# Summing the modulation over 128 rows on VectorE, by 32x32 block transposes and adds, in place of TensorE transposes

## The chip, the cores and the metric

The kernel runs on one core of a Trainium2 chip. The metric is the device time of one execution in microseconds (us), taken as the median over several runs. A profile and a trace of one further execution are at hand.

## The reference

Two transformer blocks run one after the other, each of depth 2, on 256 tokens of width 1024 in float32. The second block is conditioned: in each of its two layers a vector `c` (for the latent stream x) and a vector `c_ctx` (for the context stream h) are turned into nine modulation vectors of 1024 numbers, three for each sublayer (shift, scale and gate):

```
sc = jax.nn.silu(c)
scc = jax.nn.silu(c_ctx)
...
mod_x = (sc @ w_mod[l] + b_mod[l]).reshape(b_, N_MOD, 1, D_MODEL)
mod_h = (scc @ w_mod[l] + b_mod[l]).reshape(N_MOD, 1, D_MODEL)
...
y = adaln_in(s, g_pre, mod[..., 3 * j, :, :], mod[..., 3 * j + 1, :, :])   # rmsnorm(s) * (1 + scale) + shift
return adaln_out(s, swiglu(y, wg, wu, wd), g_post, mod[..., 3 * j + 2, :, :], FFN_RES)
```

`w_mod[l]` is 1024 x 9216. The product of a single row with it is what the change touches. Everything else (projections, attention of several kinds, SwiGLU layers) stays as it is.

## The kernel before

**The large products.** Weights come from HBM as granules of 512 KB by `nc.sync.dma_start` (tile `raw`, 4 buffers). ScalarE copies each half to a rounded float32r tile and VectorE subtracts to get the remainder (tile `hl`, 5 buffers, function `split`). TensorE multiplies in three passes (`mm3`). In the FFN of block 1 one column step is 48 matmuls of 256 columns (`mm_c`); in the FFN of block 2 the columns of both streams are mostly made together (`both`, 24 matmuls of 512 columns for gate and 24 for up). The row products are groups of `mm_f` or `mm_r`.

**The modulation.** `mod_units` makes the modulation vectors of layer `l` from column block `lo` to `hi`. For each block `i` of 1024 columns, eight tiles of `w_mod` (128 x 1024, tile `modraw`, loaded by POOL's queue into four buffers) are multiplied by a per-partition scalar and accumulated on VectorE, once for x and once for h (`part`, tile `modacc`, 128 x 1024 each, two sets). This leaves for each column 128 partial sums, one in each partition. `total` then sums over the partitions: for each half of 512 columns, four TensorE transposes into a PSUM bank (tile `mm_t`), a VectorE reduction of 128x4 from 128x512, and a VectorE add of the bias. The result lies in `modt` with the column on the partition. There are 18 blocks (4 and 5 in each layer), two streams and two halves: 72 calls of `total` and 288 transposes.

The four calls of `mod_units` are spread over the FFNs: blocks 0 and 1 of layer 0 in the FFN of block 1's first layer, blocks 2 and 3 in that of its second layer, blocks 4 to 8 in the first FFN of block 2, blocks 0 to 3 of layer 1 in its second FFN, and blocks 4 to 8 of layer 1 in its third. `fin` and `put` follow each third block. The heads of the sublayers (`pre_units`) and the rewriting of the rows' buffers wait for them.

**The order.** All work is written as units in five streams (`sx`, `sat`, `sh`, `smod`, `stot`). The function `run` plans with modelled durations (`PE_NS`, `Engine.ns`) and emits every engine's instructions in the planned order, which is then fixed. A unit with an entry in `PE_NS` takes TensorE and a PSUM bank; one without is VectorE or ScalarE work. Steps of one engine compete by class (`CLASS`): 1 if nothing else is said, 2 for the weight split, which becomes 0 when less than `SLACK` = 2500 ns of TensorE work is prepared, and 3 for `part`. In the planner's model a VectorE instruction of n elements costs 68 + n/0.96 ns. `t2k` is a ring of four buffers of 128x512 float32, used by the FFNs for the activated gate (`sg`, `gu`) and by others.

Of the kernel before, what the change touches and what calls it, by code (L numbers as in the profile page):

```python
# [11 lines left out]
F32 = mybir.dt.float32  # L12
# [3 lines left out]
ALU = mybir.AluOpType  # L16
AX = mybir.AxisListType
PSUM = bass.MemoryType.PSUM

P = 128  # L20
# [34 lines left out]
MOD_LAT = 1000.0  # L55
# [69 lines left out]
class Gran:  # L125


    def __init__(self, ap, kind):
# [7 lines left out]


PE_NS = {"col": 5760, "proj": 5760, "rope1": 5760, "half1": 2880, "half2": 2880, "wide1": 5450, "wide2": 5450, "joint": 5450, "row": 1365, "row_add": 1365, "row_last": 1365,
         "tr": 450, "total": 440, "put": 110, "rbc": 430, "start1": 30, "start2": 300, "r1": 650, "r2": 650, "r3": 430,
         "hstat": 1650, "happly": 3400, "s1": 650, "s2": 870, "s3": 650, "rope2": 860, "kcvc2": 650, "wst": 430,  # L140
         "sc2": 1730, "sc1": 870, "trp": 430, "trp2": 870, "avf": 1300, "avc": 860, "bst": 320, "gm": 1040, "bapply": 1740}
BANKS = {"row": 0, "wide1": 2, "wide2": 0, "row_add": 1, "row_last": 0, "half2": 0, "happly": 2, "sc2": 2, "bapply": 2, "trp2": 2}
# [67 lines left out]
class Chained:  # L210

    name, chained, bonus = "v", True, BONUS
# [247 lines left out]
def tile_two_blocks(ctx: ExitStack, tc, io, out):  # L460
    nc = tc.nc
    meter = Meter()
    V, A = Engine(nc.vector, "v", meter), Engine(nc.scalar, "a", meter)
    PE, G = Engine(nc.tensor, "pe", meter), nc.gpsimd
# [6 lines left out]
    sm = ctx.enter_context(tc.tile_pool(name="sm", bufs=4))  # L471
# [4 lines left out]
    ident = cst[:, C_ID:C_ID + 128]  # L476
# [5 lines left out]
    vecs = cpool.tile([P, 306], F32, name="vecs")  # L482
    V_N1, V_N2, V_RET, V_SB, V_SUB = 0, 16, 32, 40, 48
    V_C, V_PRE, V_POST, V_BM = 50, 66, 114, 162
    sc = cpool.tile([P, 2, KT], F32, name="sc")
    modt = [cpool.tile([P, 2, 72], F32, name=f"modt{l}") for l in range(DEPTH)]
# [16 lines left out]
    def t2k(shape, name):  # L503

        return wk.tile(shape, F32, tag="t2k", name=name, bufs=4)

    def t1k(shape, name):
        return wk.tile(shape, F32, tag="t1k", name=name, bufs=3)
# [4 lines left out]
    def mm_ps(shape, name):  # L513
        return ps_mm.tile(shape, F32, tag="mm", name=name)

    def st_ps(name):
        return ps_mm.tile([P, 512], F32, tag="mm", name=name)
# [440 lines left out]
    stot = Stream("tot", -2)  # L958
# [77 lines left out]
    u = sx.add("none", start0)  # L1036
# [9 lines left out]
    def mod_units(l, lo, hi, pace, after, buffers):  # L1046


        wm = io["w_mod_2"][l]
        M = {}  # L1050
        g0, g1 = 8 * lo, 8 * hi

        def load(g):
            if g < g1:
                i, k = divmod(g, 8)
                G.dma_start(M["raw"][g % len(M["raw"])], wm[k * P:(k + 1) * P, i * D:(i + 1) * D])  # L1056

        def part(g, c):
            i, k = divmod(g, 8)

            def fn():
                if g == g0 and c == 0:
                    M["raw"], M["acc"] = buffers()
                    for n in range(len(M["raw"])):
                        load(g + n)
                r = M["raw"][g % len(M["raw"])]
                if k == 0:
                    V.tensor_scalar_mul(M["acc"][i % 2][c], r, sc[:, c, k:k + 1])
                else:
                    V.scalar_tensor_tensor(M["acc"][i % 2][c], r, sc[:, c, k:k + 1], M["acc"][i % 2][c],  # L1070
                                           op0=ALU.mult, op1=ALU.add)
                if c == 1:
                    load(g + len(M["raw"]))
            return fn

        def total(i, c, e):
            def fn():
                ps = mm_ps([P, 4, P], "mm_t")
                m = modt[l][:, c, 8 * i + 4 * e:8 * i + 4 * e + 4]
                for j in range(4):  # L1080
                    PE.transpose(ps[:, j, :], M["acc"][i % 2][c][:, (4 * e + j) * P:(4 * e + j + 1) * P], ident)

                def tail():
                    yield V
                    V.tensor_reduce(m, ps, axis=AX.X, op=ALU.add)
                    at = V_BM + 72 * l + 8 * i + 4 * e
                    V.tensor_add(m, m, vecs[:, at:at + 4])
                return tail
            return fn

        def fin(j):
            cf = sm.tile([P, 2, KT], F32, tag="cf", name="cf", bufs=1)
            pre = vecs[:, V_PRE + (l * 3 + j) * 8:V_PRE + (l * 3 + j) * 8 + 8]
            post = vecs[:, V_POST + (l * 3 + j) * 8:V_POST + (l * 3 + j) * 8 + 8]
            i1, i2 = (3 * j + 1) * 8, (3 * j + 2) * 8
            for c in range(2):
                V.scalar_tensor_tensor(gain[l][c][:, j, :], modt[l][:, c, i1:i1 + 8], 1.0, pre,
                                       op0=ALU.add, op1=ALU.mult)
                V.scalar_tensor_tensor(cf[:, c, :], modt[l][:, c, i2:i2 + 8],
                                       0.5 if j != 1 else 1.0, post, op0=ALU.mult, op1=ALU.mult)  # L1100
            M["cf"] = cf

        def put(j):
            ps = st_ps("st_c")
            PE.transpose(ps[0:16, :P], M["cf"].rearrange("p c k -> p (c k)"), ident)

            def tail():
                yield A
                t = t1k([P, S], "cft")
                A.copy(t[0:16, :P], ps[0:16, :P])  # L1110
                G.dma_start(coefd[l][16 * j:16 * j + 16, :], t[0:16, :P])
            return tail

        def fin_units(j, u):
            u = stot.add("fin", lambda: fin(j), deps=[(u, 0.0)])
            return stot.add("put", lambda: put(j), deps=[(u, MOD_LAT)])

        for g in range(g0, g1):
            i, k = divmod(g, 8)
            dep = ([(u_part, 0.0)] if g > g0 else [(pace, 0.0)]) + after  # L1120
            if k == 0 and i >= lo + 2:
                dep.append((totals[l, i - 2], 0.0))
            u = smod.add("part", part(g, 0), deps=dep)
            u = u_part = smod.add("part", part(g, 1), deps=[(u, 0.0)])
            if k == 7:
                for c in range(2):
                    for e in range(2):
                        u = stot.add("total", total(i, c, e), deps=[(u, MOD_LAT)])
                totals[l, i] = u
                if i % 3 == 2:  # L1130
                    mod_done[l, i // 3] = fin_units(i // 3, u)

    def mgain(l, c, j):
        return lambda k: gain[l][c][:, j, k:k + 1]

    def mshift(l, c, j):
        return lambda k: modt[l][:, c, 24 * j + k:24 * j + k + 1]
# [314 lines left out]
    def mod_buf2():  # L1452
# [3 lines left out]
        a2 = [wk.tile([P, D], F32, tag="wt", name="modacc", bufs=4) for _ in range(2)]  # L1456
        return [r[:, 0, :], r[:, 1, :]] + r2, [[a[:, 0, :], a[:, 1, :]], a2]
    mod_units(0, 0, 2, pace0[1], [(u_s2, 0.0)], mod_buf2)
    urk.deps += ((totals[0, 1], 0.0),)
    mod_units(0, 2, 4, pace0[23], [(u_s2, 0.0)], mod_buf2)  # L1460


# [468 lines left out]
    for l in range(DEPTH):  # L1931
# [20 lines left out]
        if last:  # L1952
            at = None
            for name in SEQ[l]:
                if name in ("kb0", "kb1", "vb", "kcvc"):
                    at = gw[GRAN[name]][-1]
# [4 lines left out]
        for c, main in ((H, sh), (X, sx)):  # L1961
            mode = "sb" if c == H else "ps"
            u = pre_units(main, c, mgain(l, c, 0), mshift(l, c, 0), cur[c], [(mod_done[l, 0], 0.0)])
            coef_unit(main, l, c, 0)
            u = ffn(main, c, *ff[c][0], mode, [(u, L_TR)] + (dep[1] if c == H and l == 0 else []), pace.setdefault((l, c, 0), []),
                    joint=joints[0])
            if c == H:
                mod_units(l, 4, 9, pace[l, H, 0][MP0], [], mod_buf2)
            u = post_units(main, c, mode, u)
            u = pre_units(main, c, mgain(l, c, 1), mshift(l, c, 1), u, [(mod_done[l, 1], 0.0)])  # L1970
# [8 lines left out]
            for n_, i in enumerate(pieces):  # L1979
                def src(k, i=i, c=c):  # L1980
                    o = otile[c]
                    return o[:, 0, 2 * i + k, :], o[:, 1, 2 * i + k, :]
                u = row_units(main, c, go[c][i], src, n_ == 0, n_ == 3, "ps", [od[i]])
            att_end[l, c] = od[pieces[-1]][0]
            u = post_units(main, c, "ps", u, False, False, last)
            u = pre_units(main, c, mgain(l, c, 2), mshift(l, c, 2), u, [(mod_done[l, 2], 0.0)], last)
            coef_unit(main, l, c, 2)
            u = ffn(main, c, *ff[c][1], "ps" if last else mode, [(u, L_TR)], pace.setdefault((l, c, 1), []),
                    joint=None if last else joints[1])
# [69 lines left out]
```

## Time and profile before

| what | us |
|---|---|
| median of 3 runs | 2406.31 (2403.67 to 2406.77) |
| the profiled execution | 2403.07 |
| its span, first to last instruction | 2401.3 |

The profiled execution lies 3.2 us under the median of the runs, and its span 1.8 us under its own time. The mean granted TensorE clock of the profile is 0.994 of full speed. PE is TensorE's matmuls, DVE VectorE, ACT ScalarE, POOL GpSimd. Matmuls overlap in the pipeline, so the duration of one is longer than its distance from the next; distances between starts are what they cost.

### The profile page before, as it was taken

The numbers are of one execution on the slowest core, as the hardware profiler recorded it, in microseconds if no ns is written. First come the engines' busy times: TensorE is split into PE (matmuls) and PEld (weight loads), VectorE is DVE, ScalarE is ACT, GpSimd is POOL, SyncE is SP. The second block draws the span as 40 slices with busy tenths as digits, with TensorE's granted clock in tenths as the row PEclk, the third lists the DMA queues.
The fourth block names the chain that finished last, engine by engine and source line by source line (L and its number), as shares of the span: only waits on it lengthen the run. The fifth ranks groups of instructions, "written<-read, shape, count | busy, mean of one in ns | idle before, by whom it ended". The sixth has DMA issues, their size and how long they took to land.

```text
span 2401.3 us, 36659 instructions
## 1 busy us (share of the span) xinstructions
PE 2353.5 (98%) x14047; PEld 2072.4 (86%) x14047; DVE 1719.0 (72%) x3314; ACT 1081.1 (45%) x2271; POOL 103.8 (4%) x189
## 2 busy tenths in 40 slices
PE   8999999999999999999999999999999999998998
PEld 7999999999988888898879888888888888977997
DVE  5779767698779963574898994348998438496555
ACT  6654457544542222363576222336322226475443
POOL 1000000000001100000000100000110000000000
PEclk9999999999999999999999999999999999998999
DMA  7468665587667733443246753335775335323663
GB/s 233 149 207 268 186 182 159 169 261 219 181 187 228 220 96 97 129 128 86 74 135 197 232 171 105 97 106 184 220 219 156 93 102 175 89 72 116 190 193 115
DMA packets 455376, 385.92 MB, mean 161 GB/s; under 512 B 20608, under 2 KB 380356, under 8 KB 455200
## 3 DMA queue, kind: packets, MB, share of 16 engines
q1 hardware_dynamic: 431376, 299.67, 41.3%
q0 software_dynamic: 23648, 83.77, 11.0%
q8 instruction: 110, 1.80, 0.3%
q14 instruction: 66, 0.54, 0.1%
q10 hardware_dynamic: 176, 0.14, 0.0%
HBM read 382.43 MB, written 1.10 MB: 160 GB/s over the span
## 4 chain that ended last, share of the span: by engine, by line
PE 88%; DVE 8%; ACT 1%; issue 1%; DMA 1%; DVEq 0%; ACTq 0%
PE mm_c L206 57%; PE mm_f L206 17%; PE mm_r L206 6%; DVE hl L206 2%; PE at_s L206 1%; PE mm_t L206 1%; PE at_o L206 1%; DVE fo L206 1%; DVE res L206 1%; PE at_t L206 1%; DVE t L206 1%; PE st_rb L206 1%; DMA raw<-in_w_in_dram 1%; DVE modacc L206 1%; DVE rs_t L206 1%
## 5 line engine op out<-in xcount | busy, mean ns | idle before, releaser
L206 PE MATMUL mm_c<-yy,hl 128*128 128x256 f32 (+1 forms) x9120 | 1405.8, 314 | 10.5 <-DVE yy L206 7.5
L206 PEld LDWEIGHTS mm_c<-yy,hl 128*128 128x128 f32 x9120 | 1276.9, 192 | 117.8 <-DVE yy L206 8.9
L206 ACT CAST hl<-raw 128x512 fp32r<-128x512 f32 x1128 | 646.9, 619 | 828.1 <-issue 470.9
L206 DVE TENSOR_TENSOR hl<-raw,hl 128x512 fp32r<-128x512 f32 x1128 | 732.8, 687 | 321.6 <-ACT hl L206 320.2
L206 PE MATMUL mm_f<-hl,a 128*128 128x512 f32 x1584 | 379.4, 393 | 0.0
L206 PEld LDWEIGHTS mm_f<-hl,a 128*128 128x128 f32 x1584 | 292.4, 188 | 58.4
L206 DVE SCALAR_TENSOR_TENSOR modacc<-modraw,sc,modacc 128x1024 f32<-128x1024 f32 x252 | 313.1, 1279 | 0.0
L206 PE MATMUL mm_r<-hl,a 128*128 128x512 f32 x792 | 184.9, 390 | 0.0
L206 PEld LDWEIGHTS mm_r<-hl,a 128*128 128x128 f32 x792 | 148.2, 188 | 31.0 <-DVE hl L206 0.3
L206 ACT ACTIVATE sg<-mm_c 128x256 f32<-128x256 f32 (+1 forms) x102 | 50.0, 490 | 255.5 <-PE mm_c L206 251.7
L206 DVE TENSOR_TENSOR sg<-sg,mm_c 128x256 f32<-128x256 f32 (+1 forms) x102 | 56.4, 553 | 119.0 <-PE mm_c L206 96.1
L1056 POOL DMA_DIRECT2D modraw<-in_w_mod_dram x144 | 81.8, 569 | 978.3 <-DVE modacc L206 657.5
L206 PE MATMUL mm_f<-hl,yy 128*128 128x512 f32 x480 | 117.5, 397 | 0.0
L206 PE MATMUL mm_c<-hl,yy 128*128 128x512 f32 (+1 forms) x528 | 109.4, 364 | 0.0
L206 PEld LDWEIGHTS mm_f<-hl,yy 128*128 128x128 f32 x480 | 88.0, 188 | 20.8 <-issue 1.9
L206 PEld LDWEIGHTS mm_c<-hl,yy 128*128 128x128 f32 x528 | 89.0, 189 | 15.2 <-issue 0.7
L206 DVE TENSOR_TENSOR fo<-fo,mm_r 128x512 f32<-128x512 f32 x120 | 81.3, 683 | 11.7 <-PE mm_r L206 11.6
L206 ACT CAST a<-sg 128x256 fp32r<-128x256 f32 x154 | 57.6, 404 | 32.3 <-DVE sg L206 32.0
L206 DVE TENSOR_TENSOR a<-sg,a 128x256 fp32r<-128x256 f32 x154 | 63.6, 419 | 2.8 <-ACT a L206 2.8
L206 DVE TENSOR_TENSOR gu<-mm_c,rfac 128x512 f32<-128x512 f32 x44 | 30.3, 689 | 48.8 <-PE mm_c L206 48.7
L206 DVE TENSOR_REDUCE modt<-mm_t 128x4 f32<-128x512 f32 x72 | 49.3, 685 | 19.1 <-PE mm_t L206 18.9
L206 DVE TENSOR_REDUCE sx<-at_s 128x1 f32<-128x512 f32 (+1 forms) x72 | 40.6, 594 | 28.3 <-PE at_s L206 28.2
(196 smaller groups left out, 1375.0 us busy)
## 6 DMA issues: line engine op xcount, KB each, us to landing
modraw<-in_w_mod_dram POOLq DMA_DIRECT2D x144, 512.0 KB, 4.6
raw<-in_ffn_w_down_dram SPq DMA_DIRECT2D x100, 512.0 KB, 3.6
raw<-in_ffn_w_gate_dram SPq DMA_DIRECT2D x98, 512.0 KB, 4.5
raw<-in_ffn_w_up_dram SPq DMA_DIRECT2D x98, 512.0 KB, 4.1
raw<-in_w_in_dram SPq DMA_DIRECT2D x92, 512.0 KB, 4.8
raw<-in_w_gate_dram SPq DMA_DIRECT2D x44, 512.0 KB, 4.9
raw<-in_w_up_dram SPq DMA_DIRECT2D x44, 512.0 KB, 4.9
raw<-in_w_down_dram SPq DMA_DIRECT2D x44, 512.0 KB, 4.6
```

The source lines that it names most:

```text
L206: return f(*args, **kw)
L1056: G.dma_start(M["raw"][g % len(M["raw"])], wm[k * P:(k + 1) * P, i * D:(i + 1) * D])
```

## The change

`total` becomes a generator without TensorE work, called once for each block and stream (36 calls). For each half of 512 columns VectorE turns over the 32x32 blocks of `modacc` into a tile `mt` of the `t2k` ring, and reduces it over the 32 elements of each block to 16 columns of a small tile `mr`. Then the four groups of 32 partitions are added in two steps (64 partitions, then 32), and four adds of 32 partitions x 8 bring the sums to their partitions of `modt`, with the bias. The units are called `sums`, have no entry in `PE_NS`, and take no PSUM bank.

```diff
 PE_NS = {...
-         "tr": 450, "total": 440, "put": 110, ...
+         "tr": 450, "put": 110, ...
...
-        def total(i, c, e):
+        def total(i, c):
+
             def fn():
-                ps = mm_ps([P, 4, P], "mm_t")
-                m = modt[l][:, c, 8 * i + 4 * e:8 * i + 4 * e + 4]
-                for j in range(4):
-                    PE.transpose(ps[:, j, :], M["acc"][i % 2][c][:, (4 * e + j) * P:(4 * e + j + 1) * P], ident)
-
-                def tail():
+                a = M["acc"][i % 2][c]
+                m = modt[l][:, c, 8 * i:8 * i + 8]
+                at = V_BM + 72 * l + 8 * i
+                r = sm.tile([P, 32], F32, tag="mr", name="mr", bufs=1)
+                for e in range(2):
+                    t = t2k([P, 512], "mt")
                     yield V
-                    V.tensor_reduce(m, ps, axis=AX.X, op=ALU.add)
-                    at = V_BM + 72 * l + 8 * i + 4 * e
-                    V.tensor_add(m, m, vecs[:, at:at + 4])
-                return tail
+                    V.transpose(t, a[:, 512 * e:512 * e + 512])
+                    yield V
+                    V.tensor_reduce(r[:, 16 * e:16 * e + 16], t.rearrange("p (b i) -> p b i", i=32), axis=AX.X, op=ALU.add)
+                yield V
+                V.tensor_add(r[0:64], r[0:64], r[64:128])
+                V.tensor_add(r[0:32], r[0:32], r[32:64])
+                rv = r.rearrange("p (k q) -> p k q", q=4)
+                for q in range(4):
+                    x = slice(32 * q, 32 * q + 32)
+                    V.tensor_add(m[x], rv[0:32, :, q], vecs[x, at:at + 8])
             return fn
...
                 for c in range(2):
-                    for e in range(2):
-                        u = stot.add("total", total(i, c, e), deps=[(u, MOD_LAT)])
+                    u = stot.add("sums", total(i, c), deps=[(u, MOD_LAT)])
```

## Rows read from the trace of the kernel before

**Rows 1.** The page's first part: engine, busy us, share of the span, instructions.
```profile
PE 2353.5 (98%) x14047; PEld 2072.4 (86%) x14047; DVE 1719.0 (72%) x3314; ACT 1081.1 (45%) x2271; POOL 103.8 (4%) x189
```

**Rows 2.** Stretches: length, busy us of PE, PEld, DVE, ACT, POOL; clock, DMA share, GB/s.
```profile
165.00:290.00 125.00, 125.00 (x896) 117.97 (x895) 112.38 (x176) 58.36 (x117) 6.87 (x13) 1.00 0.77 236
290.00:345.00 55.00, 54.66 (x371) 50.47 (x370) 36.67 (x70) 29.96 (x64) 0.00 (x0) 1.00 0.62 182
...
670.00:870.00 200.00, 199.15 (x985) 167.29 (x984) 180.82 (x273) 62.50 (x126) 24.62 (x42) 1.00 0.63 195
870.00:1035.00 165.00, 165.00 (x830) 140.67 (x829) 85.84 (x169) 60.93 (x128) 3.69 (x7) 1.00 0.40 122
```

**Rows 3.** Tile mm_t: duration of one in ns (min/median/max), first and last start.
```profile
L206 PE MATMUL mm_t<-cst,modacc x288: 270/272/328, 208.0 to 1861.7; 128*128 128x128 f32 x144
```

**Rows 4.** PE in order of time, first FFN of block 2: start, us, what.
```profile
733.12 0.60 PE L206 MATMUL mm_t<-cst,modacc 128*128 128x128 f32 x4
733.48 5.75 PE L206 MATMUL mm_c<-yy,hl 128*128 128x512 f32 x24
739.06 0.60 PE L206 MATMUL mm_t<-cst,modacc 128*128 128x128 f32 x4
```

**Rows 5.** PE in order of time, FFN of block 1's first layer.
```profile
270.20 0.60 PE L206 MATMUL mm_t<-cst,modacc 128*128 128x128 f32 x4
270.56 6.00 PE L206 MATMUL mm_c<-yy,hl 128*128 128x256 f32 x48
276.40 0.60 PE L206 MATMUL mm_t<-cst,modacc 128*128 128x128 f32 x4
```

**Rows 6.** The chain that ended last: start us, us, what.
```profile
282.47 11.51 PE mm_c L206 x96
...
750.59 5.44 PE mm_c L206 x24
```

**Rows 7.** VectorE's groups, shapes apart: busy us, mean ns, idle before.
```profile
L206 DVE SCALAR_TENSOR_TENSOR modacc<-modraw,sc,modacc 128x1024 f32<-128x1024 f32 x252 | 313.1, 1279 | 0.0
...
L206 DVE TENSOR_SCALAR z<-res,rs_t 128x512 f32<-128x512 f32 x22 | 9.7, 484 | 0.4
...
L206 DVE TENSOR_REDUCE gss<-t 128x8 f32<-128x512 f32 x3 | 2.1, 686 | 0.1
```

**Rows 8.** VectorE in order of time, first FFN of block 2.
```profile
730.56 0.68 DVE L206 TENSOR_REDUCE modt<-mm_t 128x4 f32<-128x512 f32 x1
731.27 0.16 DVE L206 TENSOR_TENSOR modt<-modt,vecs 128x4 f32<-128x4 f32 x1
731.35 2.50 DVE L206 TENSOR_TENSOR hl<-raw,hl 128x512 fp32r<-128x512 f32 x4
```

**Rows 9.** Waits over the span: us in total, times, longest us.
```profile
DVE hl L206 <- ACT hl L206: 320.2, 152, 8.6
...
ACT sg L206 <- PE mm_c L206: 251.7, 36, 9.4
ACT hl L206 <- PE mm_c L206: 232.8, 84, 8.5
```

**Rows 10.** Waits of PE alone.
```profile
PE mm_y L206 <- DVE z L206: 13.0, 4, 10.5
PE mm_c L206 <- DVE yy L206: 7.5, 7, 3.2
...
PE mm_c L206 <- DVE hl L206: 0.4, 2, 0.2
```

**Rows 11.** PE in order of time, end of block 1's second FFN.
```profile
597.32 0.60 PE L206 MATMUL mm_t<-cst,modacc 128*128 128x128 f32 x4
...
608.98 1.91 PE L206 MATMUL mm_y<-cst,z 128*128 128x128 f32 x16
612.00 5.98 PE L206 MATMUL mm_c<-yy,hl 128*128 128x256 f32 x48 [1.11 <-DVE t L206]
...
662.68 11.68 PE L206 MATMUL mm_c<-yy,hl 128*128 128x256 f32 x96
```

More of the change, by code (lines that the diff above doesn't have):

```diff
@@ L138 @@
 PE_NS = {"col": 5760, "proj": 5760, "rope1": 5760, "half1": 2880, "half2": 2880, "wide1": 5450, "wide2": 5450, "joint": 5450, "row": 1365, "row_add": 1365, "row_last": 1365,
-         "tr": 450, "total": 440, "put": 110, "rbc": 430, "start1": 30, "start2": 300, "r1": 650, "r2": 650, "r3": 430,
+         "tr": 450, "put": 110, "rbc": 430, "start1": 30, "start2": 300, "r1": 650, "r2": 650, "r3": 430,
          "hstat": 1650, "happly": 3400, "s1": 650, "s2": 870, "s3": 650, "rope2": 860, "kcvc2": 650, "wst": 430,
```

## The prediction

> **What bounds the kernel now.** I read the page's first part, then the busy time by stretches over the places where the modulation runs, then the tile `mm_t`, then the timelines of TensorE and VectorE there, and last the waits. The first part says that TensorE is busy 2353.5 of 2401.3 us and VectorE 1719.0 [rows 1]. That is an average, so the stretches decide. Where the modulation runs, both engines are nearly full: in 165 to 290 us TensorE is busy for all 125 us and VectorE for 112.4; in 670 to 870 us it is 199.2 and 180.8 of 200 [rows 2]. The reader is to see that TensorE has no gap in which its transposes could be free, and that VectorE has little room in the very stretches where it is to get more work. Right behind these two it has room: 85.8 busy of 165 us in 870 to 1035 and 36.7 of 55 in 290 to 345 [rows 2]. So VectorE is full because `part` has the lowest class and fills whatever is left, not because the FFN needs it full. The waits confirm which engine sets the pace: TensorE waited 0.4 us in the whole span for a VectorE half of a weight split, while ScalarE's half of the split waited 232.8 us for TensorE to give weight buffers back [rows 9, 10].
>
> **What TensorE loses.** 288 transposes in 72 groups of four [rows 3]. One takes 272 ns by its own duration, but they overlap, so I price a group by what it adds to the distance between two starts. In the FFN of block 2, from one group to the next with 24 matmuls of 512 columns between is 739.06 - 733.12 = 5.94 us [rows 4]; 24 such matmuls alone are 5.44 us [rows 6]. A group costs 0.50 us. In the FFN of block 1, a group and 48 matmuls of 256 columns are 276.40 - 270.20 = 6.20 us [rows 5], 48 alone are half of 11.51, 5.755 us [rows 6]: 0.445 us. Four of the 18 column blocks lie in block 1 (16 groups), 14 in block 2 (56 groups): 16 x 0.445 + 56 x 0.50 = 7.1 + 28.0 = 35.1 us. The bounds are 72 x 0.445 = 32.0 and 72 x 0.50 = 36.0. The PSUM bank of each group is free as well; no wait in the rows is for a bank, so I count nothing for it.
>
> At 0.50 us for four, a transpose costs TensorE 0.125 us. The Trainium skill ("VectorE: DVE Perf Modes", The three transpose paths) gives 390 ns for a 128x128 bf16 transpose on TensorE and 311 ns on VectorE, and under Rules for kernel authors it sends 128x128 transposes to TensorE where PSUM will do, which speaks against this change. By its figures, as an estimate, 288 x 0.390 = 112 us would leave TensorE; the trace shows under a third of that, because these run in a full pipeline, and the measurement decides.
>
> **What VectorE gains in work.** Before, a group cost a reduction and an add: 731.35 - 730.56 = 0.79 us until the next instruction [rows 8], two for each of the 36 pairs of block and stream, 1.58 us. After, a pair has two block transposes, two reductions and six small adds.
> - The reductions read SBUF instead of PSUM. Such a reduction of 512 elements takes 686 ns [rows 7] against 0.68 us from PSUM [rows 8], so nothing changes but the count of outputs.
> - A block transpose doesn't stand in the trace. From below, a one-input instruction of 128x512 takes 484 ns; from above, an instruction of 1024 elements takes 1279 ns, as if each element passed twice [rows 7]. I take 0.69 us, the duration of the other 512-element instructions, to which it is nearest in size.
> - An instruction that needs the one before starts 0.03 us after its end (730.56 + 0.68 to 731.27), one that doesn't starts 0.08 us before its end (731.27 + 0.16 to 731.35) [rows 8]. So transpose, reduction, transpose, reduction are 0.72 + 0.61 + 0.72 + 0.72 = 2.77 us. The adds are 0.16 us each; two form a chain, and for all six I take 0.19 us: 1.14 us. If the last four overlap, at 0.08 us, it is 0.70.
>
> The pair comes to 3.91 us, 2.33 more than before: 84 us of VectorE over 36 pairs. With the low transposes (two at 0.51, reductions at 0.61 and 0.72, adds 0.70) it is 3.05, that is 53 us more in all; with the high ones (two at 1.31, 0.61, 0.72, 1.14) 5.10, that is 127 us more.
>
> **Why I cost that at nothing.** It falls as 4 pairs (9 us) in each of the two FFNs of block 1 and as 10, 8 and 10 pairs (23, 19, 23 us) in those of block 2. It takes precedence over `part`, which is pushed back by as much, and the last block is finished later by that. What is late next: after the first stretch the buffers of `modacc` and `modraw` are wanted again near 345 us, with 18 us of VectorE idle before; after the third, the next sublayer's head at about 1032 us, with 79 us idle. Both hold even at the high price (14 and 35 us). The second has the least room: its last group is at 597.32 and the context stream's head transposes follow at 608.98, at whose columns TensorE waits 1.11 us at 612.00 [rows 11]. Nine us later for that head costs nothing as long as TensorE has columns of block 1 to do, which it has until 662.68 [rows 11]; if the plan leaves a hole there, it is of the size of that 1.11 us.
>
> If the cover goes, the weight split is what is late, then TensorE. The split is class 2 against 1 for the new steps, but turns to 0 when less than 2.5 us of matmuls is prepared, and the new work yields after every large instruction, so a split waits for one of them, or for the six small adds (1.1 us). With five weight buffers of some 5.44 us each [rows 6] TensorE has about 20 us ahead of it.
>
> The tile `mt` takes two of the four `t2k` buffers in turn with `sg` and `gu`. The first writer of `sg` is ScalarE, so a late reduction can hold its activation, and behind it ScalarE's half of the splits. ScalarE waits 251.7 us for TensorE before these activations [rows 9], so a us here and there is covered; I take 0, with 2 us as the other end. DMA: modulation loads are issued when `part` releases a buffer, so they come later, not more often.
>
> The planner's order changes everywhere, also in the attention stages that have no modulation. What a reshuffle can move is the size of the existing holes: 13.0 us before the head transposes, 7.5 before the columns [rows 10]. I take 0 and put 4 us on either side.
>
> **The sum.** Profiled execution: 2403.1 - 35.1 = 2368.0, span 2366.2. The runs' median lies 3.2 us above the profiled execution, so 2406.3 - 35.1 = 2371.2: I predict 2371. Its own range: 36.0 + 4 of reshuffle and 2 for the spread of the runs down, 2364; 32.0 with 4 + 2 against it, 2380.
>
> **The rivals.**
> - Part of the gain is lost to VectorE running behind its plan. The planner prices the pair at 4 x 0.60 + 6 x 0.08 = 2.9 us (68 + n/0.96 ns each), I at 3.9; before it was 1.35 against 1.58. That is 0.8 us more lag for each pair, 8 us in a stretch of ten pairs, 28 in all, in an engine with no idle time to catch up. If all of it reached TensorE the gain is 7 us (2399); half of it, 21 us (2385). For it: VectorE's fullness [rows 2]. Against it: 20 us of prepared weights, and 0.4 us of such waits so far.
> - No difference: TensorE's time comes back as waits elsewhere, for weights (the DMA share is 0.77 at 236 GB/s in the first stretch [rows 2]) or in a reshuffled attention stage. It needs 30 us of new holes, more than all of the 20.9 us in the rows [rows 10]. 2402 to 2411.
> - Slower: VectorE becomes the bound in the stretches of the modulation. All 84 us there would give 2406 + 84 - 35 = 2455; it decides once more than 35.1 / 84 = 42% of the added time reaches TensorE, about 1 us for each pair. For it: the stretches at 670 to 870 and the two like it are full. Against it: the lowest-class work gives way first, and the idle time behind it holds it all. The skill's rule above, that such transposes belong on TensorE, points this way: by its 311 ns a block, 288 blocks are 90 us where I have 50, still under my high end.
>
> **Chances.** The forecast 0.72, a partial gain 0.13, no difference 0.06, slower 0.09. A difference under 0.2% (4.8 us) can't be told from none here. Faster is 0.72 + 0.13 = 0.85, same 0.06, slower 0.09. For 8 in 10 the range takes the forecast's own and the nearer half of the partial case: 2362 to 2388.
>
> **What the profile after would show.** TensorE has 576 fewer instructions over matmuls and weight loads; no `mm_t`; groups of 24 joint matmuls follow at 5.44 us throughout the stretches; VectorE busy rises by 50 to 125 us; the `modacc` transposes read 0.5 to 0.8 us; the last `modt` of each stretch comes 10 to 25 us later against TensorE's work; TensorE's waits for `hl` stay under 2 us. I am wrong if those waits grow by tens of us, if the block transpose is over 1.3 us, or if the holes of the attention stages grow.

## The result and the profile after

| | us |
|---|---|
| before, median of 4 | 2404.99 |
| after, median of 4 | 2379.56 (2378.88 to 2381.55) |
| ratio | 0.9895, 95% interval 0.9884 to 0.9907 |
| profiled execution after, its span | 2381.55, 2379.8 |

The change makes the kernel faster, by 25.4 us. The prediction had 35.1. The time lies in the range, and at the upper edge of the likeliest case's own range of 2364 to 2380. Where the other 10 us went is the question of the experiments.

The page's first part after, to be read against [rows 1]:

```profile
PE 2321.8 (98%) x13759; PEld 2043.5 (86%) x13759; DVE 1788.3 (75%) x3530; ACT 1083.5 (46%) x2271; POOL 103.8 (4%) x189
```

TensorE has 288 matmuls fewer and VectorE 69 us more. The groups of VectorE, shapes apart (busy us, mean ns, idle before), show what those are:

```profile
L206 DVE STREAM_TRANSPOSE mt<-modacc 128x512 f32<-128x512 f32 x72 | 50.9, 707 | 0.0
L206 DVE TENSOR_REDUCE mr<-mt 128x16 f32<-128x512 f32 x72 | 49.2, 684 | 1.7
L206 DVE TENSOR_TENSOR modt<-mr,vecs 32x8 f32<-32x8 f32 x144 | 22.7, 158 | 2.7
L206 DVE TENSOR_TENSOR mr<-mr 64x32 f32<-64x32 f32 x36 | 6.7, 187 | 1.2
L206 DVE TENSOR_TENSOR mr<-mr 32x32 f32<-32x32 f32 x36 | 6.5, 180 | 1.2
```

A block transpose of 128x512 takes 707 ns, near the 0.69 us that were taken between bounds of 0.48 and 1.28. What the block transposes cost is therefore not where the forecast missed. TensorE's waits after, against [rows 10] (us in total, times, longest):

```profile
PE mm_y L206 <- DVE z L206: 12.9, 4, 10.5
PE mm_c L206 <- DVE yy L206: 7.5, 7, 3.2
...
PE mm_c L206 <- DVE hl L206: 4.0, 5, 1.0
PE st_c L206 <- DVE cf L206: 3.6, 3, 1.2
PE mm_r L206 <- DVE sg L206: 2.8, 5, 1.3
...
PE mm_c L206 <- DVE fo L206: 0.9, 2, 0.5
```

The first two are as before. The last four are new or grown, and all four name VectorE work. They lie in the stages with modulation, except for 1.1 us of the waits for `hl`, which fall in the first 14 us of the span, where there were 0.4 before. Two of the stretches of [rows 2], in the same columns:

```profile
670.00:870.00 200.00, 196.19 (x923) 163.85 (x922) 185.97 (x302) 63.94 (x128) 21.82 (x38) 1.00 0.63 194
870.00:1035.00 165.00, 164.56 (x839) 140.57 (x839) 106.74 (x214) 65.18 (x140) 4.14 (x8) 1.00 0.43 130
```

TensorE is idle for 3.81 us of the first where it was idle for 0.85. VectorE's work moves into the second, 106.7 us for 85.8, which has the room. TensorE's busy time counts the last matmul before a wait with its whole duration, which is longer than its distance from a next one would be, so the idle time understates the loss.

To see where the gain is made and lost, the two traces can be laid beside each other at instructions that both have. The PE rows in order of time at those points, after:

```profile
40.18 0.86 PE L206 MATMUL at_z<-skq 128*128 128x256 f32 x4
...
358.70 0.82 PE L206 MATMUL at_z<-skq 128*128 128x256 f32 x4
...
1036.92 0.60 PE L206 MATMUL at_w<-cst,wsr 128*128 128x128 f32 x4
...
2028.60 0.60 PE L206 MATMUL at_w<-cst,wsr 128*128 128x128 f32 x4
```

And before:

```profile
37.99 0.86 PE L206 MATMUL at_z<-skq 128*128 128x256 f32 x4
...
358.85 0.82 PE L206 MATMUL at_z<-skq 128*128 128x256 f32 x4
...
1044.87 0.60 PE L206 MATMUL at_w<-cst,wsr 128*128 128x128 f32 x4
...
2050.06 0.60 PE L206 MATMUL at_w<-cst,wsr 128*128 128x128 f32 x4
```

| stretch between the points | modulation in it | predicted | measured |
|---|---|---|---|
| start to the first attention | none | 0 | +2.2 |
| to the second layer's attention | 8 groups in block 1 | -3.6 | -2.3 |
| to the first attention of block 2 | 8 in block 1, 20 in block 2 | -13.6 | -7.8 |
| to the second attention of block 2 | 36 in block 2 | -18.0 | -13.5 |
| to the end of the span | none | 0 | 0.0 |

"Predicted" is the groups of transposes by 0.445 and 0.50 us; "measured" the change of the distance between the points. The start of the profiled execution came 2.2 us later, and it was the slowest of the four: before any modulation, TensorE's waits for `rs_t` and `hl` are 1.5 and 0.7 us longer. Apart from that, nothing changes in the last stretch, which has no modulation, and each stretch with modulation keeps between 57% and 75% of what was predicted: together 23.6 of 35.1 us. 11.5 us are lost inside these stages, about what the last four waits above sum to there (10.2 us).

### The profile page after: what moved, and what is told of

Same layout as the page of the kernel before. It is cut to its first block, busy times and chain, and to the rows that moved or that the text cites. A ratio compares the mean times of both kernels' runs of the same rounds, so it can differ in the third digit from the quotient of the medians.

```text
span 2379.8 us, 36302 instructions
## 1 busy us (share of the span) xinstructions
PE 2321.8 (98%) x13759; PEld 2043.5 (86%) x13759; DVE 1788.3 (75%) x3530; ACT 1083.5 (46%) x2271; POOL 103.8 (4%) x189
## 5 line engine op out<-in xcount | busy, mean ns | idle before, releaser
L206 PE MATMUL mm_f<-hl,a 128*128 128x512 f32 x1584 | 371.1, 390 | 0.0
L206 DVE STREAM_TRANSPOSE mt<-modacc 128x512 f32<-128x512 f32 x72 | 50.9, 707 | 0.0
```

Source lines behind the costliest of these rows:

```text
L206: return f(*args, **kw)
```

## The experiments

Three theories, stated before the runs. **Lag:** the planner `run` fixes every engine's order with modelled durations, in which a pair of sums costs 2.9 us (4 instructions of 0.60, two small adds of 0.10, four of 0.08); it takes 4.1 on the chip. VectorE falls behind the plan by 1.2 us for each pair, and TensorE, whose order is fixed too, meets operands that the plan thought ready. **Precedence:** the sums' class puts them ahead of the FFN's steps, and the plan knows that it is late. **Ring:** ScalarE's activations wait for the `t2k` buffers that the block transposes hold; the trace after has one such wait, of 6.6 us. Before all of these stands the question whether the term of 35.1 us was right at all.

Each run has its own comparison with the kernel before on the same chip: 2403.44 us for the first four, 2404.76 for the other four.

**x1, no sums.** The whole computation of the sums is left out.

```diff
-                for e in range(2):
-                    t = t2k([P, 512], "mt")
...
                 yield V
...
-                    V.tensor_add(m[x], rv[0:32, :, q], vecs[x, at:at + 8])
+                V.tensor_add(m, a[:, 0:8], vecs[:, at:at + 8])
```

> The sums over the 128 rows are left out (each pair of block and stream does one add of 128x8, so the modulation is wrong), neither TensorE nor VectorE does their work. All theories: this shows the whole of what the old sums cost, so it checks the term of 35.1 us. If that term is right, the time is 2370 us (2366 to 2374), some 10 us under the changed kernel; then the missing 10 us are paid by the new work on VectorE. If TensorE's transposes were in truth worth only 25 us, it stays at 2378 to 2381, where the changed kernel is.

Measured: 2367.47 us, ratio 0.9849 (0.9834 to 0.9863), 36.0 us less. The old sums were worth what was predicted, and 2367 us, the time of this kernel without them, is the floor against which the other runs are read.

**x2, true prices.** The instructions are those of the change; only the planner is told what they take.

```diff
                     V.transpose(t, a[:, 512 * e:512 * e + 512])
+                    meter.op("v", 140.0)
                     yield V
                     V.tensor_reduce(r[:, 16 * e:16 * e + 16], t.rearrange("p (b i) -> p b i", i=32), axis=AX.X, op=ALU.add)
+                    meter.op("v", 120.0 * e)
...
                     V.tensor_add(m[x], rv[0:32, :, q], vecs[x, at:at + 8])
+                meter.op("v", 800.0)
```

> The changed kernel with nothing altered but what the planner is told a pair of sums costs: 4.1 us, as measured, in place of 2.9. Theory lag (VectorE runs behind the planned order, because the planner's prices are too low, and TensorE meets operands that the plan thought ready): 5 to 10 us faster than the changed kernel, 2370 to 2375, and the 1.2 us holes before the coefficients' transposes go. Theory precedence (the sums stand in front of the gate's product by their class, and the plan knows it): within 2 us of the changed kernel. Theory ring (ScalarE's activation waits for the buffer that the block transposes use): within 2 us.

Measured: 2368.41 us (2368.32 to 2368.95), ratio 0.9853 (0.9839 to 0.9868), 35.0 us less than before and 0.9 from the floor. Precedence and ring had nothing to offer here. The place where it can be seen is the first block of the first FFN of block 2. VectorE in order of time in the changed kernel, from the end of the second pair of sums:

```profile
731.17 0.67 DVE L206 TENSOR_TENSOR modt<-mr,vecs 32x8 f32<-32x8 f32 x4
731.93 2.50 DVE L206 TENSOR_TENSOR hl<-raw,hl 128x512 fp32r<-128x512 f32 x4
734.35 1.28 DVE L206 SCALAR_TENSOR_TENSOR modacc<-modraw,sc,modacc 128x1024 f32<-128x1024 f32 x1
735.54 0.68 DVE L206 TENSOR_TENSOR sg<-sg,mm_c 128x512 f32<-128x512 f32 x1
...
745.20 0.69 DVE L206 TENSOR_TENSOR sg<-sg,mm_c 128x512 f32<-128x512 f32 x1
```

and TensorE there:

```profile
724.06 16.48 PE L206 MATMUL mm_c<-yy,hl 128*128 128x512 f32 x72
740.38 4.24 PE L206 MATMUL mm_r<-hl,a 128*128 128x512 f32 x18
745.94 1.67 PE L206 MATMUL mm_r<-hl,a 128*128 128x512 f32 x6 [1.32 <-DVE sg L206]
748.08 5.74 PE L206 MATMUL mm_c<-yy,hl 128*128 128x512 f32 x24 [0.47 <-DVE fo L206]
```

The first 24 `mm_c` end near 729.5 (724.06 + 5.44), and the gate's product `sg`, which needs them, starts at 735.54, 6.0 us later: four splits and a modulation product stand in front of it. The next `sg` comes at 745.20, 4.8 us after its matmuls end, and now the row products run into it: their last six wait 1.32 us, and the matmuls behind them wait for a PSUM bank that VectorE's `fo` add empties late. The same place with true prices:

```profile
727.65 0.67 DVE L206 TENSOR_TENSOR modt<-mr,vecs 32x8 f32<-32x8 f32 x4
728.41 0.69 DVE L206 TENSOR_TENSOR hl<-raw,hl 128x512 fp32r<-128x512 f32 x1
729.02 0.68 DVE L206 TENSOR_TENSOR sg<-sg,mm_c 128x512 f32<-128x512 f32 x1
...
736.98 5.60 PE L206 MATMUL mm_r<-hl,a 128*128 128x512 f32 x24
...
739.29 0.68 DVE L206 TENSOR_TENSOR sg<-sg,mm_c 128x512 f32<-128x512 f32 x1
```

The sums stand at the same place, ahead of the gate's product, but only one split follows them before it. The product starts 2.9 us after its matmuls (720.66 + 5.44 to 729.02), the next one 2.3 us, and the 24 row products run through. The planner had filled the time that it thought free. TensorE's waits for `cf` and `sg` are gone from the list, those for `hl` fall from 4.0 to 3.0 us, and ScalarE's waits for `sg` fall back from the first of these rows to the second (before they were 32.0):

```profile
ACT a L206 <- DVE sg L206: 91.8, 41, 5.6
```

```profile
ACT a L206 <- DVE sg L206: 30.7, 21, 5.6
```

**x3, twice the error.** Again the same instructions.

```diff
                     V.transpose(t, a[:, 512 * e:512 * e + 512])
+                    meter.op("v", -460.0)
                     yield V
                     V.tensor_reduce(r[:, 16 * e:16 * e + 16], t.rearrange("p (b i) -> p b i", i=32), axis=AX.X, op=ALU.add)
+                    meter.op("v", -140.0)
```

> The same instructions as in the changed kernel, but the planner is told 1.2 us less for each pair (1.7 us), so that the error is doubled. Theory lag: the loss against the plan grows by as much again, 5 to 12 us slower than the changed kernel, 2385 to 2392. Theories precedence and ring: within 3 us of the changed kernel.

Measured: 2425.22 us, ratio 1.0092 (1.0077 to 1.0107). This is slower than the kernel before, by 21.8 us, and far more than expected: against the truly priced order an error of 1.2 us for each pair costs 10 us, one of 2.4 costs 57. TensorE's waits in this run:

```profile
PE mm_r L206 <- DVE sg L206: 18.1, 7, 3.5
PE mm_y L206 <- DVE z L206: 17.0, 5, 10.5
PE st_c L206 <- DVE cf L206: 15.4, 6, 4.3
```

(13.0 us of the second row are old.) The direction is that of the lag theory alone. The size says that the loss isn't proportional to the error. The engines' busy time in this run, and below it in x2, shows what it is made of:

```profile
PE 2335.3 (96%) x13759; PEld 2051.3 (85%) x13759; DVE 1792.5 (74%) x3530; ACT 1082.3 (45%) x2271; POOL 103.3 (4%) x189
```

```profile
PE 2317.5 (98%) x13759; PEld 2042.2 (86%) x13759; DVE 1789.2 (76%) x3530; ACT 1082.7 (46%) x2271; POOL 102.0 (4%) x189
```

The spans are 2424.0 and 2366.7 us, 57.3 apart. TensorE is idle for 39.5 us more, and the same 13759 matmuls are busy for 17.8 us more. The second part goes with TensorE's clock: added up over stretches of 4 us, what the granted clock falls short of full speed comes to 33 us in this trace and to 14 in that of x2, an estimate of 19 us more. In the second FFN of block 2, with modulation, the columns of [rows 2] are

```profile
1290.00:1460.00 170.00, 160.97 (x828) 138.53 (x827) 167.35 (x280) 60.11 (x125) 17.09 (x30) 0.95 0.65 200
```

with a granted clock of 0.95, where x2 has 1.00 and the changed kernel 0.99. In that stretch six row products wait 3.46 us for `sg`, until 1407.67 us. From 1408 to 1412 us the granted clock is 0.50, the lower of TensorE's two levels (1.2 GHz), and the six take 2.93 us, where the six behind the wait of 1.32 us in the changed kernel took 1.67.

**x4, the sums in class 3.**

```diff
 CLASS = {"part": 3,
...
+         "sums": 3,
```

> The changed kernel with the sums in class 3, that of the modulation's products, in place of 1, so that weight splits and the FFN's own VectorE steps go before them. Theory precedence: 5 to 10 us faster than the changed kernel, 2370 to 2375. Theory lag: 0 to 4 us faster, since the error of the prices stays. Theory ring: no difference or slower, since the buffers are held longer.

Measured: 2383.75 us (2378.04 to 2384.66), ratio 0.9911 (0.9895 to 0.9928). No gain over the changed kernel, against either expectation. TensorE's waits for the coefficients, which need the last sums, grow from 3.6 us, those for the gate's product stay (3.4 for 2.8), and those for `hl` fall back to 0.4. The helper's line is L207 here, for the line added above it:

```profile
PE st_c L207 <- DVE cf L207: 7.8, 5, 2.0
```

So the class alone isn't the cause: the weight splits come in time, the coefficients come later, and nothing is won. Moved back, the sums still carry the wrong price.

**x5, too high a price.** The true prices and 0.6 us more for each block transpose; the edit is shown against x2.

```diff
-                    meter.op("v", 140.0)
+                    meter.op("v", 740.0)
```

> As the run with true prices, but each block transpose is told to cost 0.6 us more than it does, 1.2 us more for each pair of sums (5.3 us). Theory lag: once the price is no lower than the cost, a higher one brings nothing and costs little, so within 4 us of the truly priced kernel, 2366 to 2373. Theory luck (any change of the prices reshuffles the order, and the truly priced one came out well by chance): anywhere from 2370 to 2400.

Measured: 2368.30 us, ratio 0.9851 (0.9836 to 0.9865). With the price 1.2 us too high the time is that of the true price to 0.1 us, so x2 wasn't a lucky order.

**x6, only the small adds priced.**

```diff
                     V.tensor_add(m[x], rv[0:32, :, q], vecs[x, at:at + 8])
+                meter.op("v", 800.0)
```

> The changed kernel with only the part of the missing price that belongs to the six small adds (0.8 of the 1.2 us for each pair). Theory lag, if it is the sum of the error that counts: two thirds of the 11 us come back, 2371 to 2374. If the block transposes' and reductions' error of 0.4 us is what hurts: 2377 to 2381.

Measured: 2370.30 us (2368.63 to 2371.49), ratio 0.9857 (0.9843 to 0.9872). That is 34.5 us less than before: two thirds of the error removed give back 9 of the 10 us. These two thirds lie in the six smallest instructions of the change. Since the loss isn't proportional to the error, the run doesn't show that an error there hurts more than the same error elsewhere; no run priced the block transposes and reductions alone.

**x7, a tile of their own.** The block transposes get the third buffer of the ring whose other two hold `modraw`.

```diff
-                    t = t2k([P, 512], "mt")
+                    t = M["mt"][:, 512 * e:512 * e + 512]
...
         a2 = [wk.tile([P, D], F32, tag="wt", name="modacc", bufs=4) for _ in range(2)]
+        mt = wk.tile([P, D], F32, tag="p", name="mt", bufs=3)
```

> The changed kernel with the block transposes in a tile of their own (the third buffer of the ring that holds two of the loaded modulation tiles) instead of two buffers of the activations' ring; prices as in the changed kernel. Theory ring: 2 to 6 us faster than the changed kernel, 2373 to 2377, and ScalarE's wait of 6.6 us for the block transposes' tile is gone. Theory lag: that wait is gone and the time stays within 2 us, 2377 to 2381.

Measured: 2380.91 us, ratio 0.9902 (0.9886 to 0.9919), as the changed kernel. ScalarE's wait of 6.6 us for `mt` is gone and nothing is won by it. In the truly priced kernel that wait is even longer:

```profile
ACT sg L206 <- DVE mt L206: 9.1, 1, 9.1
```

The ring costs nothing.

**x8, the kernel before with truer prices.**

```diff
                     V.scalar_tensor_tensor(M["acc"][i % 2][c], r, sc[:, c, k:k + 1], M["acc"][i % 2][c],
                                            op0=ALU.mult, op1=ALU.add)
+                    meter.op("v", 60.0)
...
                     V.tensor_add(m, m, vecs[:, at:at + 4])
+                    meter.op("v", 120.0)
```

> The kernel before with two prices made true: each modulation product 0.06 us more and each old sum's VectorE part 0.12 us more. Theory lag: the kernel before also runs behind its plan (some 15 us over all products) but with next to no waits for it, so no gain: 2400 to 2406. If the true prices alone were worth the 11 us, whatever engine makes the sums, it falls to 2392 to 2396.

Measured: 2402.74 us, ratio 0.9993 (0.9984 to 1.0002). The kernel before doesn't gain by it, so the 35 us of x2 come from the change of engine and not from better prices by themselves.

The six kernels that make the sums by block transposes with the class unchanged, by the error of the price for one pair:

| price minus cost, us for a pair | -2.4 (x3) | -1.2 (the change) | -1.2 (x7) | -0.4 (x6) | 0 (x2) | +1.2 (x5) |
|---|---|---|---|---|---|---|
| time, us | 2425.2 | 2379.6 | 2380.9 | 2370.3 | 2368.4 | 2368.3 |

The version to keep is x2. It beats both kernels: 35.0 us under the one before and, through the two comparisons, some 10 us under the change.

## Why the prediction was right, and where it was short

- **TensorE's term** was right: 35.1 predicted, 36.0 measured when the old sums are simply left out, 35.0 when VectorE makes them without lag. Pricing four transposes by the distance between starts, and not by their durations of 272 ns, is what made it so.
- **VectorE's added work** was right: a pair takes 4.0 to 4.1 us from its first instruction to what follows it, for the 3.9 taken, so some 90 us for the 84 predicted, and the 72 block transposes take 50.9 us for the 50 taken. Busy time rises by 69 only, in part since it leaves out the short waits between dependent instructions. Where it was put, behind each stretch, is also right: 870 to 1035 us takes up 20.9 us.
- **"I cost that at nothing"** is the step that failed. True with the right prices (x2 against x1: 0.9 us), it was false in the kernel as changed, by some 10 us. The prediction named the mechanism as a rival, priced the lag at 0.8 us for each pair, gave a gain of 21 us for half of it reaching TensorE, and a chance of 0.13. The lag is 1.2 us for a pair, about 1.0 more than the old sums' (2 x 0.12), and the part that reached TensorE is 11.5 of 36 x 1.2 = 43 us, about a quarter. What I held against it, 20 us of prepared weights, is no cover for most of what came late. That the time still lies in the forecast's own range, by 0.4 us, is luck: this range was made of TensorE's term, the reshuffle and the spread of the runs, and has no lag in it.
- **What is late next** was right in the smaller part: "the weight split is what is late, then TensorE". Of the 10.2 us of waits in the stages with modulation, those for the split's `hl` are 2.9. The rest are the gate's product `sg`, for which the row products wait, the coefficients `cf`, whose transposes stand in TensorE's fixed order, and the `fo` add. The sign that these `hl` waits stay under 2 us failed, with 4.0 over the span.
- **The ring, the reshuffle, the deadlines** were rightly costed at nothing or nearly so: x7 shows it for the first; for the second the last stretch does, which has no modulation and changes by 0.0 us. As to the deadlines, the tightest one, the end of block 1's second FFN, has 1.9 us of waits for `hl` (600 to 603 us) in place of the 1.11 us for `t` [rows 11].
- **The rivals on the other side.** "Slower" didn't happen, but x3 shows that it was near: the same instructions with 1.2 us more of planning error in each pair are 21.8 us slower than before. The cause isn't that rival's, VectorE as the bound: VectorE has the same work in x2.

## What to carry to other kernels

In a kernel whose order is planned from modelled durations and then fixed, a new kind of instruction has to be given its true duration together with the change; an engine that the plan holds full has no idle time in which an error can heal. Small dependent instructions are the ones to look at first, since a model by element count can miss most of what they take (here 0.5 us was planned for six adds that take 1.1). And when an engine gains cheap-looking work, ask which operand of the bottleneck stands behind it in that engine's queue, and not only whether there is idle time somewhere.

## What the runs showed of the hardware that was not expected

- The four adds into `modt` don't depend on each other and yet don't overlap: four take 0.67 us with 0.158 us each, 0.17 us from start to start, while in [rows 8] an independent instruction starts 0.08 us before the small add ahead of it ends. Each of the four writes to another group of 32 partitions. The Trainium skill ("VectorE: DVE Perf Modes", Two Vector instructions with no wait between them) says, as a model, that an instruction which starts in another such group than the last one reading or writing that memory starts only when all earlier ones have finished. The trace agrees, with these 0.17 us; no run here tried the adds within one group.
- The block transpose of 128x512 float32 takes 707 ns where a two-input subtraction of the same length (`hl`) takes 688: turning the blocks over is hardly dearer than arithmetic on them.
